# Strassen's seven block products for the output projection of a two-layer decoder trunk

## Chip, cores and metric

The kernel runs on one core of a Trainium2 chip. The metric is the device time of one launch in microseconds; the median of three runs of the kernel before is 1445.24 us. Its hardware profile is of one more execution, which took 1446.19 us.

## What is computed

Two layers of a hybrid decoder trunk on 1024 tokens with 1024 channels, all in float32: a norm, one wide input projection, sliding-window attention with sinks and a gated linear recurrence beside each other, a gated merge, an output projection and a residual addition; then a final norm. What matters here is the end of each layer:

```
merged = (jax.nn.sigmoid(gate_attn) * (a @ w_up_attn[layer])
          + jax.nn.sigmoid(gate_hgrn) * (b @ w_up_hgrn[layer]))
x = x + merged @ w_out[layer]
...
return rms_norm(x, final_norm_w)
```

`a` and `b` are 1024 x 512 each, `merged` is 1024 x 1024, `w_out[layer]` 1024 x 1024.

## The kernel before

Every large product is computed in a split form: an operand is rounded by ScalarE to a shorter float (`hi`, a cast to float32r), VectorE subtracts to get the rest (`lo`), and TensorE adds three products, lo x hi, hi x lo and hi x hi, into one accumulator. So a product costs three matmuls for each block of 128 of the contraction, and each operand piece costs one cast on ScalarE and one subtraction on VectorE. `split_w` (L125) writes the two parts into buffers with two copies each, `split_slot` (L333) into slots. There are 40 slots of 4 KB per partition (`slot`, tag "slot"), which most tiles of the kernel share. Accumulators come from two pools of PSUM banks: three under the tag "pj", five under "bank". Loads and most stores are issued by SyncE's queue, in order.

The kernel is written in a framework that inserts the semaphores and orders each engine's instructions itself: the order of the program text is the priority, and work that is ready earlier may go ahead of work that stands before it.

The input projection already uses seven block products (`combine`, `pair_first`, `pair_rest`). Its results for the gates are written through the activation to the DRAM tensor `gd`. While the recurrence runs, `filling` (L1039) feeds TensorE with independent work, the last part of which is `up_attn` (L811): for pairs of 128 output channels it computes `a @ w_up_attn` for both halves of the tokens, copies the accumulators to `u1` with ScalarE, loads the first branch's gates (`gate_in`) and multiplies on VectorE.

The merge (L1073 to L1089) then runs over four pairs of channel blocks: it loads and splits the weights of the second up projection (`up_chunk`, L788), loads the second gates into `u2`, and for each channel block and each half of the tokens computes 12 matmuls (`up`, L793), multiplies the accumulator by the gate (L802), adds `u1` (L1084), and writes `hi` (L1086) and `lo` (L1087) into `mg`. `mg[a][k]` is half `a` of the tokens, channel block `k`, with channels on partitions: the stationary operand of the output projection.

The output projection differs between the layers. In both, an accumulator holds 128 tokens x 512 output channels and sums 8 channel blocks, thus 24 matmuls:

- Layer 0 (L1143 to L1174): for each half of the tokens and each half of the output channels, four accumulators are open; pieces of `w_out` of 256 rows are loaded, split, and used by all four. Each piece of `w_out` is loaded and split twice, once for each half of the tokens. Then the residual is added (L1168), and the rows are stored to `xd`. The first half's norm for the next layer (`norm_scale`, `norm_turn`: squares on ScalarE, a short chain and a scaling on VectorE, transposes on TensorE, copies, casts and low parts) stands after the first two accumulations of the second half, and three chunks of the next layer's input weights (`first_chunk`) are loaded within it.
- Layer 1 (L1098 to L1142): all of `w_out` is split once. After a first round over the four first blocks, each block of 128 tokens is completed in turn (`part`, L1102), its residual added and squared (`add`, L1112), and `finish` (L1119) computes the final norm's factor, scales and stores.

Of the kernel before, what the change touches and what calls it, by code (L numbers as in the profile page):

```python
# [10 lines left out]
F32 = mybir.dt.float32  # L11
# [6 lines left out]
P = 128  # L18
# [20 lines left out]
def trunk_kernel(ctx, tc, x, positions, norm_w, w_in, attn_sinks, hgrn_norm_w, w_up_attn,  # L39
# [432 lines left out]
    for L in range(DEPTH):  # L472
# [331 lines left out]
        def gate_in(c, nm):  # L804
            t = slot([P, T], nm)
            nc.sync.dma_start(t, gd[c * P:(c + 1) * P])
            return t
# [3 lines left out]
        def up_attn(m, asp):  # L811
            w = up_chunk(w_up_attn[L], m, f"ua{L}_{m}")
            u1.extend(slot([P, T], f"u1_{L}_{m + j}") for j in range(2))
            n = 0
            for j in range(2):
                for a in range(2):
                    up(a, j, w, asp, u1[m + j][:, a * 512:(a + 1) * 512], f"ua{L}_{m + j}_{a}", True)
# [5 lines left out]
            for j in range(2):  # L823
                t = gate_in(m + j, f"ga_{L}_{m + j}")
                V.tensor_tensor(out=u1[m + j], in0=u1[m + j], in1=t, op=ALU.mult)
# [247 lines left out]
        mg = [[None] * KT for _ in range(2)]  # L1073
        u2s = []
        for m in range(0, KT, 2):
            w = up_chunk(w_up_hgrn[L], m, f"uh{L}_{m}")
            u2s += [gate_in(KT + c, f"u2_{L}_{c}") for c in range(len(u2s), min(m + 4, KT))]
            u2 = u2s[m:m + 2]
            for j in range(2):
                for a in range(2):  # L1080
                    t = slice(a * 512, (a + 1) * 512)
                    u = u2[j][:, t]
                    up(a, j, w, bsp, u, f"uh{L}_{m + j}_{a}")
                    V.tensor_tensor(out=u, in0=u, in1=u1[m + j][:, t], op=ALU.add)  # L1084
                    g = slot([P, 2, 512], f"mg_{L}_{m + j}_{a}", F32R)
                    S.copy(g[:, 0], u)  # L1086
                    V.tensor_tensor(out=g[:, 1], in0=u, in1=g[:, 0].bitcast(F32), op=ALU.subtract)  # L1087
                    mg[a][m + j] = g


        last = L == DEPTH - 1

        def load_wo(n, nm):
            return split_rows(w_out[L], n * 512, 512, f"o{L}_{n}_{nm}", 0 if n else 4)

        if last:
            wo = [load_wo(0, "l")]
            xns = [load_x(b, L) for b in range(4)]  # L1098
            wo.append(load_wo(1, "l"))
            wb = bcast_row(final_norm_w, "fnw")  # L1100

            def part(b, n, acc, ks):  # L1102
                a, o = b // 4, (b % 4) * P
                for k in ks:
                    lh, ll = mg[a][k][:, 0, o:o + P], mg[a][k][:, 1, o:o + P]
                    PE.matmul(acc, lhsT=ll, rhs=wo[n][k][0], start=k == 0, stop=False)
                    PE.matmul(acc, lhsT=lh, rhs=wo[n][k][1], start=False, stop=False)
                    PE.matmul(acc, lhsT=lh, rhs=wo[n][k][0], start=False, stop=k == KT - 1)

            sums = {}  # L1110

            def add(b, n, acc):  # L1112
                xn = xns[b][:, n * 512:(n + 1) * 512]
                V.tensor_tensor(out=xn, in0=acc, in1=xn, op=ALU.add)
                if n == 0:
                    sums[b] = st.tile([P, 2], F32, tag="fs", name=f"fs_{b}", bufs=5)
                S.activation(junk[:, n * 512:(n + 1) * 512], xn, AF.Square, accum_out=sums[b][:, n:n + 1])

            def finish(b):  # L1119
# [96 lines left out]
```

## Time and profile before

| | |
|---|---|
| median of 3 runs | 1445.24 us (1443.05 to 1448.75) |
| profiled execution | 1446.19 us, of which the span of instructions is 1444.4 us |
| TensorE busy | 1415.8 us, 98% of the span |
| VectorE busy | 922.1 us, 64% |
| ScalarE busy | 691.1 us, 48% |
| merge, layer 0 / layer 1 | 598 to 641 us / 1305.6 to 1349 us |
| output projection, layer 0 / layer 1 | 641 to 733 us / 1349 to 1437.1 us |
| after the last matmul | 1437.1 to 1444.4 us |

In rows of groups, a line number is that of the kernel printed above; then come the engine, the operation, the tile written and the tiles read, the shape and the count, and behind the bar the busy time in us, the mean duration of one in ns, and the idle time of the engine just before them with what ended it. In rows of instructions in order of time, the first number is the start and the second the duration in us; what stands in brackets is the idle time before and what ended it. PE is TensorE, PEld its weight loads, DVE VectorE, ACT ScalarE, POOL GpSimd, SP SyncE. The time of a matmul overlaps that of the next.

### The profile page before, as it was taken

Reading aid. Unit: us, or ns where it says so; the run is one execution under the profiler, and the core shown is the slowest. Engines: PE = TensorE matmul, PEld = TensorE weight load, DVE = VectorE, ACT = ScalarE, POOL = GpSimd, SP = SyncE. Lnnn points to the kernel's source line nnn. Section 1 sums busy time; section 2 is a strip of 40 time slices with the busy share of each in tenths; the row PEclk is TensorE's granted clock in tenths of the full one; section 3 lists DMA queues with packets and bytes.
Section 4 is the critical chain, followed back from the end, with each engine's and each line's share of the span. In section 5 each row is a group of like instructions: output and inputs, shape, how many; then the busy total and the mean of one; then the engine's idle time right before and its main releaser. Section 6 shows DMA issues by size and latency. Waiting matters only on the chain.

```text
span 1444.4 us, 21317 instructions
## 1 busy us (share of the span) xinstructions
PE 1415.8 (98%) x8252; PEld 1149.4 (80%) x8252; DVE 922.1 (64%) x1560; ACT 691.1 (48%) x1382; POOL 68.6 (5%) x77
## 2 busy tenths in 40 slices
PE   8999999999999999999999999999999999999997
PEld 7877878878777878888888878887788778888886
DVE  5856756646645889673656466666456388978643
ACT  8754333245775644432556332333467655453321
POOL 1100000310000000000000000003000000000000
PEclk9999999999999999999999999999999999999999
DMA  8433443464236653355455343426523366443431
GB/s 271 155 109 124 142 151 123 145 164 133 71 113 202 218 190 130 139 181 170 156 199 154 102 131 124 142 92 199 170 77 105 125 206 225 155 174 133 144 134 59
DMA packets 194277, 214.35 MB, mean 148 GB/s; under 512 B 12480, under 2 KB 142016, under 8 KB 194176
## 3 DMA queue, kind: packets, MB, share of 16 engines
q1 hardware_dynamic: 161152, 161.59, 35.1%
q10 hardware_dynamic: 31488, 46.15, 8.7%
q0 software_dynamic: 1536, 5.24, 0.9%
q8 instruction: 65, 1.06, 0.3%
q14 instruction: 36, 0.29, 0.1%
HBM read 145.58 MB, written 59.77 MB: 142 GB/s over the span
## 4 chain that ended last, share of the span: by engine, by line
PE 78%; DVE 7%; ACT 6%; DMA 5%; issue 2%; SPq 0%; ACTq 0%; DVEq 0%
PE pb L291 4%; PE pb L293 4%; PE pb L292 4%; PE pg L263 3%; PE pg L265 3%; PE pc L291 3%; PE pg L264 3%; PE pc L293 2%; PE pc L292 2%; PE pj_qh L139 2%; PE pj_qh L141 2%; PE pj_qh L140 2%; PE av L746 2%; PE pj_f L139 2%; PE pj_f L140 2%; PE pj_f L141 2%
## 5 line engine op out<-in xcount | busy, mean ns | idle before, releaser
L128 ACT CAST whi_s<-ws 128x1024 fp32r<-128x1024 f32 x26 | 27.4, 1054 | 123.3 <-DVE ws L278 108.4
L706 DVE COPY_PREDICATED pr<-upper,sc 128x256 f32<-128x256 int32 x56 | 23.4, 444 | 51.6 <-ACT pr L705 43.9
L721 ACT ACTIVATE pr<-pr,mx 128x128 f32<-128x128 f32 x128 | 50.1, 396 | 5.0 <-DVE mx L718 4.0
L139 PE MATMUL pu_ua<-wh_a,wlo_ua 128*128 128x512 f32 x128 | 52.2, 408 | 0.0
L141 PE MATMUL pu_ua<-wh_a,whi_ua 128*128 128x512 f32 x128 | 50.7, 396 | 0.0
L1164 PE MATMUL po<-wlo_o,mg 128*128 128x512 f32 x128 | 49.9, 390 | 0.7 <-DVE wlo_o L129 0.7
L483 ACT ACTIVATE pq<-pq 128x512 f32<-128x512 f32 x60 | 37.7, 631 | 26.3 <-DVE pq L303 25.1
L263 PE MATMUL pg<-hh,wlo_p 128*128 128x512 f32 (+1 forms) x128 | 47.0, 372 | 3.3 <-POOL wlo_p L129 1.5
L140 PE MATMUL pu_ua<-wl_a,whi_ua 128*128 128x512 f32 x128 | 50.2, 392 | 0.0
L1163 PE MATMUL po<-whi_o,mg 128*128 128x512 f32 x128 | 49.9, 390 | 0.0
L1165 PE MATMUL po<-whi_o,mg 128*128 128x512 f32 x128 | 49.8, 389 | 0.0
L139 PE MATMUL pu_uh<-wh_b,wlo_uh 128*128 128x512 f32 x128 | 49.8, 389 | 0.0
L140 PE MATMUL pu_uh<-wl_b,whi_uh 128*128 128x512 f32 x128 | 49.8, 389 | 0.0
L141 PE MATMUL pu_uh<-wh_b,whi_uh 128*128 128x512 f32 x128 | 49.8, 389 | 0.0
L303 DVE TENSOR_TENSOR pq<-pb,p 128x512 f32<-128x512 f32 x40 | 27.6, 690 | 31.9 <-PE pb L293 31.8
L264 PE MATMUL pg<-hl,whi_p 128*128 128x512 f32 (+1 forms) x128 | 46.1, 363 | 0.0
L265 PE MATMUL pg<-hh,whi_p 128*128 128x512 f32 (+1 forms) x128 | 46.0, 363 | 0.0
L1086 ACT CAST mg<-u 128x512 fp32r<-128x512 f32 x32 | 19.8, 621 | 51.3 <-DVE u L1084 51.3
L277 DVE TENSOR_TENSOR ws<-wr 128x512 f32<-128x512 f32 x26 | 17.9, 690 | 39.5 <-DMA wr<-in_w_in_dram 39.5
L263 PE MATMUL pg<-hh,wl_p 128*128 128x512 f32 (+1 forms) x112 | 41.2, 369 | 1.8 <-DVE wl_p L337 1.2
L291 PE MATMUL pb<-th,wl 128*128 128x512 f32 x104 | 41.3, 397 | 1.7 <-DVE pq L303 1.7
L129 DVE TENSOR_TENSOR wlo_t<-ws,whi_t 128x1024 fp32r<-128x1024 f32 x26 | 31.8, 1223 | 16.5 <-ACT whi_t L128 16.5
(391 smaller groups left out, 4432.6 us busy)
## 6 DMA issues: line engine op xcount, KB each, us to landing
wr<-in_w_in_dram SPq DMA_DIRECT2D x64, 512.0 KB
gd<-pq ACTq DMA_DIRECT2D x76, 256.0 KB
wr_p<-in_w_in_dram SPq DMA_DIRECT2D x26, 512.0 KB
fq<-fq ACTq DMA_DIRECT2D x48, 256.0 KB
x<-in_x_dram SPq DMA_DIRECT2D x16, 512.0 KB
ga<-gd SPq DMA_DIRECT2D x16, 512.0 KB
u<-gd SPq DMA_DIRECT2D x16, 512.0 KB
wr_o<-in_w_out_dram SPq DMA_DIRECT2D x16, 512.0 KB
```

What stands on the lines that cost most here:

```text
L139: PE.matmul(acc, lhsT=ll, rhs=rh, start=i == 0, stop=False)
L140: PE.matmul(acc, lhsT=lh, rhs=rl, start=False, stop=False)
L141: PE.matmul(acc, lhsT=lh, rhs=rh, start=False, stop=i == n - 1)
L263: PE.matmul(acc, lhsT=wl[:, k], rhs=h[:, t], start=k == 0, stop=False, skip_group_check=q > 0)
L264: PE.matmul(acc, lhsT=wh[:, k], rhs=l[:, t], start=False, stop=False, skip_group_check=q > 0)
L265: PE.matmul(acc, lhsT=wh[:, k], rhs=h[:, t], start=False, stop=k % 4 == 3, skip_group_check=q > 0)
L291: PE.matmul(acc, lhsT=wl[:, k], rhs=h, start=start and k == 0, stop=False, skip_group_check=not start)
L292: PE.matmul(acc, lhsT=wh[:, k], rhs=l, start=False, stop=False, skip_group_check=not start)
L293: PE.matmul(acc, lhsT=wh[:, k], rhs=h, start=False, stop=k == 3, skip_group_check=not start)
L721: S.activation(pr[:, h], pr[:, h], AF.Exp, bias=mx[:, h:h + 1], accum_out=sm[:, h:h + 1])
L1163: PE.matmul(accs[j], lhsT=ll, rhs=wh[:, i], start=k + i == 0, stop=False)
L1164: PE.matmul(accs[j], lhsT=lh, rhs=wl[:, i], start=False, stop=False)
```

## The change

The output projection of both layers becomes one routine. The merged matrix A (tokens x channels) and W = `w_out` are cut into halves both ways, and the four blocks of the result are formed from seven products of 512 x 512 blocks in Winograd's arrangement, with the sums S1 = A21 + A22, S2 = S1 - A11, S3 = A11 - A21, S4 = A12 - S2 and T1 = B12 - B11, T2 = B22 - T1, T3 = B22 - B12, T4 = T2 - B21 (up to sign and order of writing). (The code writes S3 as A22 - S2, and T4 as B21 - T2.) Each product takes four row blocks, four channel blocks and three matmuls each, 48 matmuls. Products go in the order 1, 2, 6, 5, 3, 7, 4 and accumulate in two sets of four banks, X and Y; the residual rows are added from a bank after each stage that completes a term of an output block (`add`), so that a block of the output is built up in `xns` by several additions, and X or Y goes on accumulating.

The sums are VectorE operations on tiles of 128 x 1024, in place. Operands are split when their product comes up: the left ones into slots, the right ones into the two buffers of `split_w`, but for product 4, whose right operand goes to slots and whose matmuls run block by block, so that each block's rows are complete at the block's end. `w_out` is loaded once as eight tiles of 256 rows x 512 columns, during the merge.

In the merge, `up` writes into tiles of two channel blocks x 512 tokens; the addition of the two branches is one operation for two channel blocks; no split is made there. The multiplication of `u1` by the first branch's gates moves from `up_attn` into the merge, with its loads, and both kinds of gates are loaded by half of the tokens.

In layer 0, the first half's norm now stands ahead of product 4, and two of the three early weight chunks behind it. In layer 1, the first four blocks are finished ahead of product 4 (`finish_block`), the other four within it. The list `weighed` is empty, so both halves of a block are scaled by VectorE.

```
--- before.py
+++ after.py
 
 
-        def up_chunk(w, m, nm):
+        def up_load(w, m, nm):
             raw = wp.tile([P, 4, 2 * P], F32, tag="wraw", name=f"wr_{nm}")
             nc.sync.dma_start(raw, w[:, m * P:(m + 2) * P].rearrange("(k p) c -> p k c", p=P))
-            return split_w(raw, nm, [P, 4, 2 * P])
+            return raw
+
+        def up_chunk(w, m, nm):
+            return split_w(up_load(w, m, nm), nm, [P, 4, 2 * P])
 
         def up(a, j, w, src, dst, nm, wait=False):
 
...
-            nc.sync.dma_start(t, gd[c * P:(c + 1) * P])
+        def gate_in(c, a, nm):
+
+            t = slot([P, 2, 512], nm)
+            nc.sync.dma_start(t, gd[c * P:(c + 2) * P].rearrange("(j p) t -> p j t", p=P)[:, :, a * 512:(a + 1) * 512])
             return t
 
         u1 = []
 
         def up_attn(m, asp):
             w = up_chunk(w_up_attn[L], m, f"ua{L}_{m}")
-            u1.extend(slot([P, T], f"u1_{L}_{m + j}") for j in range(2))
+            u1.append([slot([P, 2, 512], f"u1_{L}_{m}_{a}") for a in range(2)])
             n = 0
             for j in range(2):
                 for a in range(2):
-                    up(a, j, w, asp, u1[m + j][:, a * 512:(a + 1) * 512], f"ua{L}_{m + j}_{a}", True)
+                    up(a, j, w, asp, u1[m // 2][a][:, j], f"ua{L}_{m + j}_{a}", True)
                     n += 1
                     if n == 1:
                         yield
                     elif n == 2:
                         yield
-            for j in range(2):
-                t = gate_in(m + j, f"ga_{L}_{m + j}")
-                V.tensor_tensor(out=u1[m + j], in0=u1[m + j], in1=t, op=ALU.mult)
             yield
 
...
-        mg = [[None] * KT for _ in range(2)]
+
+        mg = [[], []]
         u2s = []
+        last = L == DEPTH - 1
+
+        def w_block(q, n):
+
+            res = []
+            for kp in (2 * q, 2 * q + 1):
+                t = slot([P, 2, 512], f"wo_{L}_{n}_{kp}")
+                nc.sync.dma_start(t, w_out[L][kp * 2 * P:(kp + 1) * 2 * P, n * 512:(n + 1) * 512]
+                                  .rearrange("(k p) c -> p k c", p=P))
+                res.append(t)
+            return res
+
+        wo = {}
+        raws = [up_load(w_up_hgrn[L], 0, f"uh{L}_0")]
         for m in range(0, KT, 2):
...
+            w = split_w(raws.pop(0), f"uh{L}_{m}", [P, 4, 2 * P])
+            if m + 2 < KT:
+                raws.append(up_load(w_up_hgrn[L], m + 2, f"uh{L}_{m + 2}"))
+            for c in range(2 * len(u2s), min(m + 4, KT), 2):
+                u2s.append([(gate_in(KT + c, a, f"u2_{L}_{c}_{a}"), gate_in(c, a, f"ga_{L}_{c}_{a}")) for a in range(2)])
+            for a in range(2):
+                u, t = u2s[m // 2][a]
+                V.tensor_tensor(out=t, in0=t, in1=u1[m // 2][a], op=ALU.mult)
+                for j in range(2):
+                    up(a, j, w, bsp, u[:, j], f"uh{L}_{m + j}_{a}")
+                V.tensor_tensor(out=u, in0=u, in1=t, op=ALU.add)
+                mg[a].append(u)
+            if m:
+                for q, n in (((0, 0),), ((0, 1), (1, 0)), ((1, 1),))[m // 2 - 1]:
+                    wo[q, n] = w_block(q, n)
+
...
+        a11, a12, a21, a22 = mg[0][:2], mg[0][2:], mg[1][:2], mg[1][2:]
+        b11, b12, b21, b22 = wo[0, 0], wo[0, 1], wo[1, 0], wo[1, 1]
+        X = [pj.tile([P, 512], F32, tag="pj", name=f"px_{L}_{j}") for j in range(3)] + [bank([P, 512], f"px_{L}_3")]
+        xns = []
+        def sums(out, in0, in1, op):
+            for o, i0, i1 in zip(out, in0, in1):
+                V.tensor_tensor(out=o, in0=i0, in1=i1, op=op)
+        def split_a(a, nm):
+            return [split_slot(t, f"m{L}_{nm}_{i}", [P, 2, 512]) for i, t in enumerate(a)]
+        def product(acc, a, w, nm, start, by_block=False, first=None):
+            ws = []
+            for kp in range(2):
+                ws.append(w[kp] if by_block else split_w(w[kp], f"o{L}_{nm}_{kp}", [P, 2, 512]))
+                for j in [] if by_block else range(4):
+                    times(acc[j], a[kp], ws[kp], j, start, kp)
+            for j in range(4) if by_block else []:
+                first(j)
+                for kp in range(2):
+                    times(acc[j], a[kp], ws[kp], j, start, kp)
+                yield j
+        def times(acc, a, w, j, start, kp):
+            for i in range(2):
+                lh, ll = a[0][:, i, j * P:(j + 1) * P], a[1][:, i, j * P:(j + 1) * P]
+                PE.matmul(acc, lhsT=ll, rhs=w[0][:, i], start=start and kp + i == 0, stop=False,
+                          skip_group_check=not start)
+                PE.matmul(acc, lhsT=lh, rhs=w[1][:, i], start=False, stop=False, skip_group_check=not start)
+                PE.matmul(acc, lhsT=lh, rhs=w[0][:, i], start=False, stop=kp + i == 2, skip_group_check=not start)
+        def run(*args):
+            for _ in product(*args):
+                pass
+        ssq, weighed = {}, []
+        def add(acc, a, n, done=False, js=range(4)):
+            for j in js:
+                b = 4 * a + j
                 xn = xns[b][:, n * 512:(n + 1) * 512]
+                V.tensor_tensor(out=xn, in0=acc[j], in1=xn, op=ALU.add)
+                if last and done:
+                    if b not in ssq:
+                        ssq[b] = st.tile([P, 2], F32, tag="fs", name=f"fs_{b}", bufs=8)
+                    S.activation(junk[:, n * 512:(n + 1) * 512], xn, AF.Square, accum_out=ssq[b][:, n:n + 1])
+        def finish_block(b):
+            V.tensor_tensor(out=ssq[b][:, 0:1], in0=ssq[b][:, 0:1], in1=ssq[b][:, 1:2], op=ALU.add)
+            r = rsqrt(ssq[b][:, 0:1], 1, 1.0 / D, f"fin_{b}", True)
+            for n in range(2):
+                c = slice(n * 512, (n + 1) * 512)
+                if n and b in weighed:
+                    S.activation(xns[b][:, c], xns[b][:, c], AF.Copy, scale=r)
+                else:
                     V.scalar_tensor_tensor(out=xns[b][:, c], in0=xns[b][:, c], scalar=r, in1=wb[:, c],
                                            op0=ALU.mult, op1=ALU.mult)
+                nc.sync.dma_start(out[0, b * P:(b + 1) * P, c], xns[b][:, c])
+        m11 = split_a(a11, "11")
+        run(X, m11, b11, "1", True)
+        xns += [load_x(b, L) for b in range(4)]
+        m12 = split_a(a12, "12")
+        Y = [bank([P, 512], f"py_{L}_{j}_0") for j in range(4)]
+        run(Y, m12, b21, "2", True)
+        sums(a21, a21, a22, ALU.add)
+        sums(a11, a21, a11, ALU.subtract)
+        sums(b11, b12, b11, ALU.subtract)
+        t2 = [slot([P, 2, 512], f"t2_{L}_{i}") for i in range(2)]
+        sums(t2, b22, b11, ALU.subtract)
+        add(X, 0, 0)
+        m = split_a(a11, "s2")
+        run(X, m, t2, "6", False)
+        sums(a12, a12, a11, ALU.subtract)
+        add(Y, 0, 0, True)
+        xns += [load_x(b, L) for b in range(4, NB)]
+        m = split_a(a21, "s1")
+        Y = [bank([P, 512], f"py_{L}_{j}_1") for j in range(4)]
+        run(Y, m, b11, "5", True)
+        add(X, 0, 1)
+        if last:
+            wb = bcast_row(final_norm_w, "fnw")
         else:
             wb = bcast_row(norm_w[L + 1], f"nw_{L + 1}")
             hT, hF, early = HT(f"{L + 1}"), Turned(f"{L + 1}"), []
+        m = split_a(a12, "s4")
+        add(Y, 1, 1)
+        run(Y, m, b22, "3", False)
+        sums(b12, b22, b12, ALU.subtract)
+        sums(a11, a22, a11, ALU.subtract)
+        m = split_a(a11, "s3")
+        run(X, m, b12, "7", False)
+        sums(b21, b21, t2, ALU.subtract)
+        m22 = split_a(a22, "22")
+        w4 = split_a(b21, "t4")
+        add(Y, 0, 1, True)
+        if not last:
+            early.append(first_chunk(L + 1, 0, True))
+            for b in range(4):
+                nc.sync.dma_start(xd[b * P:(b + 1) * P], xns[b])
+            norm_turn(norm_scale(xns[:4], wb, f"n{L + 1}_0"), hT, hF, 0, f"n{L + 1}_0")
+        if last:
+            for b in range(4):
+                finish_block(b)
+        for j in product(X, m22, w4, "4", False, True, lambda j: add(X, 1, 1, True, [j])):
+            add(X, 1, 0, True, [j])
+            if last:
+                finish_block(4 + j)
+            else:
+                nc.sync.dma_start(xd[(4 + j) * P:(5 + j) * P], xns[4 + j])
+        if not last:
+            early += [first_chunk(L + 1, j, True) for j in (1, 2)]
+            xnl = xns[4:]
```

More of the change, by code (lines that the diff above doesn't have):

```diff
@@ L1070, in trunk_kernel @@
             pass
-        mg = [[None] * KT for _ in range(2)]
+        mg = [[], []]
         u2s = []
-        for m in range(0, KT, 2):
[L1076 to L1088, printed above, removed]
```

73 lines of the change are left out of this document (removed).

## Prediction

> **What bounds the kernel now.** I read the shares of the engines first, then the stretches around the change (layer 0 and layer 1: merge, output projection, what follows), then the order of TensorE's instructions, and last what VectorE does there.
>
> ```profile
> PE 1415.8 (98%) x8252; PEld 1149.4 (80%) x8252; DVE 922.1 (64%) x1560; ACT 691.1 (48%) x1382; POOL 68.6 (5%) x77
> PE 78%; DVE 7%; ACT 6%; DMA 5%; issue 2%; SPq 0%; ACTq 0%; DVEq 0%
> ```
>
> ```profile
> 598.00:641.00 43.00, 43.00 (x191) 35.59 (x190) 36.64 (x52) 14.19 (x22) 0.00 (x0) 1.00 0.42 135
> 641.00:733.00 92.00, 91.30 (x420) 75.79 (x419) 46.44 (x58) 35.39 (x54) 0.00 (x0) 1.00 0.51 164
> 1305.60:1349.00 43.40, 43.40 (x193) 35.92 (x193) 36.82 (x53) 14.42 (x22) 0.00 (x0) 1.00 0.29 97
> 1349.00:1437.10 88.10, 87.45 (x385) 71.78 (x383) 37.41 (x82) 21.35 (x46) 0.00 (x0) 1.00 0.35 126
> 1437.10:1444.40 7.30, 0.00 (x0) 0.00 (x0) 3.06 (x9) 0.93 (x3) 0.00 (x0) 0.72 0.19 72
> ```
>
> The columns are length, then busy time of PE, PEld, DVE, ACT, POOL, the granted clock, the DMA share and GB/s. Rows one and three are the two merges, two and four the two output projections, five the end. TensorE is busy throughout all four, at clock 1.00; VectorE is busy 85% of a merge, but only 50% and 42% of the projections. So TensorE is the bound, and VectorE has half of the projections free. That free half is what the change spends.
>
> A matmul's 389 ns overlaps the next one's, so its price is the distance between starts:
>
> ```profile
> 701.06 0.39 PE L1164 MATMUL po<-wlo_o,mg 128*128 128x512 f32 x1
> 707.41 0.39 PE L1165 MATMUL po<-whi_o,mg 128*128 128x512 f32 x1
> 707.64 3.65 PE L225 MATMUL tp_n<-ident,x 128*128 128x128 f32 x32
> 711.05 0.48 PE L1163 MATMUL po<-whi_o,mg 128*128 128x512 f32 x1
> ```
>
> 28 steps in 6.35 us: 0.227 us each. A projection has 384 (8 row blocks, 2 column halves, 8 blocks of the contraction, 3 terms of the split), thus 87.05 us. From 641.3 to 732.7 the first projection takes 91.4; less 87.05 and the 3.4 of 32 transposes that sit in it (707.64 to 711.05), about 1.0 is idle.
>
> ```profile
> L1106 PE MATMUL po<-whi_o_l,mg x32: 389/389/389, 1349.0 to 1428.1; 128*128 128x512 f32 x32
> L1108 PE MATMUL po<-wh_o_l,mg x96: 388/389/398, 1360.3 to 1436.7; 128*128 128x512 f32 x96
> L1163 PE MATMUL po<-whi_o,mg x128: 389/389/476, 641.3 to 732.2; 128*128 128x512 f32 x128
> ```
>
> The second runs from 1349.0 to 1436.9, 87.9, with 0.9 idle.
>
> **The change part by part.** **Matmuls removed.** Seven products of 4 row blocks x 4 blocks of the contraction x 3 terms are 336 instead of 384: 48 fewer per layer, 96 in all, of the same 128x512 shape with a weight load each. 96 x 0.227 = -21.8 us, all on the path. The Trainium skill (TensorE: Matmul & The Clock Gate, "Wait — 56ns, not 53.3ns?") gives 215.7 ns start to start for such a matmul; that would be -20.7, and the row above decides for 0.227.
>
> **VectorE work added to the projection.** The rows for the prices:
>
> ```profile
> 756.55 1.22 DVE L337 TENSOR_TENSOR wl_p<-wr_p,wh_p 128x1024 fp32r<-128x1024 f32 x1
> 757.68 1.22 DVE L241 TENSOR_TENSOR h<-h,h 128x1024 f32<-128x1024 f32 x1
> 758.82 1.22 DVE L240 TENSOR_TENSOR h<-h,h 128x1024 f32<-128x1024 f32 x1
> L1168 DVE TENSOR_TENSOR x<-po,x 128x512 f32<-128x512 f32 x16 | 10.7, 687 | 5.6 <-PE po L1165 5.6
> L128 ACT CAST whi_o<-wr_o 128x1024 fp32r<-128x1024 f32 x16 | 17.0, 1060 | 46.6 <-PE po L1165 33.4 <-DMA wr_o<-in_w_out_dram 12.1 <-PE pu_uh L141 1.1
> ```
>
> A 128x1024 subtraction or sum lasts 1.22, but where nothing is awaited the next one starts 1.14 later; I take 1.15. Per layer: 14 operand pieces of each side (seven products, two tiles each) make 28 low parts; eight sums of two tiles make 16; together 44 x 1.15 = 50.6. Seven sets of four additions from PSUM are 28 x 0.66 = 18.5. Sum 69. Three of the first product's four low parts fit in the merge. ScalarE gets 28 casts x about 1.0 = 28 for a projection of 76 us, and is no bound.
>
> Set against this, product by product, with 0 at the first product (10.9 us each on TensorE, order 1, 2, 6, 5, 3, 7, 4). The hard point is the third: products 1 and 2 last 21.8 us, and before product 6 VectorE owes two low parts of a12, two of b21, eight sums and two low parts of S2, one of T2 (15 x 1.15 = 17.3) and four additions from PSUM (2.6): 19.9. The last merge operand comes some 2 us late (0.69 + 1.22 behind the last matmul), so 19.9 stand against 19.8, less what went ahead in the merge (a12's pieces come free before its end). Products 5, 3 and 7 owe less than the 10.9 of one product each: four low parts with two sums and four additions, with eight additions, or with four sums are 9.2 to 9.9, and the sums can go ahead. Up to product 4 I take +1.5 per layer for stalls at operands; bounds 0 and, if the third product waits for its chain in a row (two sums, a cast and a low part, 1.23 + 1.23 + 1.06 + 1.23), 4.8.
>
> Weight pieces keep two buffers each, freed per half product (24 matmuls, 5.4 us); cast and low part take 2.3 of that. w_out is now read once (8 loads of 512 KB, not 16, in layer 0), ahead of use, and the waits for it go: the 1.0 and 0.9 idle above, -1.9.
>
> **Merge.** It loses 16 additions and 16 low parts of 128x512 (about 21 us by these rows):
>
> ```profile
> L1084 DVE TENSOR_TENSOR u<-u,u 128x512 f32<-128x512 f32 x16 | 10.9, 688 | 0.3
> L1087 DVE TENSOR_TENSOR mg<-u,mg 128x512 fp32r<-128x512 f32 x16 | 10.9, 688 | 3.7 <-ACT mg L1086 3.4
> L825 DVE TENSOR_TENSOR u<-u,ga x16: 1209/1214/1220, 542.9 to 1309.3; 128x1024 f32<-128x1024 f32 x16
> ```
>
> and gains eight wide additions and eight gate products (16 x 1.15 = 18.4): no more than now, and under the 43.4 of its matmuls. Six of the eight gate products per layer came before the merge, where TensorE was busy too; nothing is gained by their leaving (0; bound -1 per layer). Their loads (4 MB) move into the merge with w_out's 4 MB, 4 MB of the second gates and 2 MB of weights: at most 14 MB in 43 us, 325 GB/s, and less as the first gates go ahead of it. In the stretch 1200 to 1445, in slices of 6.1 us:
>
> ```profile
> GB/s 255 228 375 53 80 217 175 248 268 3 0 96 319 101 6 371 312 31 58 102 155 196 64 86 2 226 402 114 364 163 104 88 86 0 86 39 49 86 0 86
> ```
>
> Single slices reach 371 and 402, so I take 0 and keep 3 per layer as the bound. On SyncE's queue these loads stand behind waits for weight buffers, which come free every 10.9 us; two groups of gates go ahead.
>
> **End of layer 0.** The first half's norm now has its inputs only after product 3, two products (21.8 us) before the projection ends; so far its transposes ran 21 us before the end with inputs ready at 685. Ahead of product 4 VectorE owes one weight piece, a chain of 12 short operations and four scalings:
>
> ```profile
> 689.32 0.16 DVE L108 TENSOR_SCALAR ms_n<-ss_n 128x4 f32<-128x4 f32 x1
> 691.71 3.67 DVE L170 SCALAR_TENSOR_TENSOR x<-x,y_n,nw 128x1024 f32<-128x1024 f32 x3
> 696.69 1.27 DVE L170 SCALAR_TENSOR_TENSOR x<-x,y_n,nw 128x1024 f32<-128x1024 f32 x1
> L231 ACT CAST hh<-h 128x1024 fp32r<-128x1024 f32 x8 | 8.1, 1186 | 0.0
> L232 DVE TENSOR_TENSOR hl<-h,hh 128x1024 fp32r<-128x1024 f32 x8 | 9.3, 1220 | 11.5 <-ACT hh L231 11.5
> ```
>
> Product 3 ends at 54.5, squares to 60, short chain to 62.5, scalings to 67.5; product 7 ends at 65.3, the transposes (3.4) fill to about 68.7, and the additions that free product 4's accumulators come at 67.5 to 68. +1.0, bounds 0 and 5 (all scalings exposed). Copies, casts and low parts are done by 77, product 4 at 80: layer 1 starts without a gap. Its second half is needed only some 60 us later.
>
> **End of layer 1.** The finishing of a block:
>
> ```profile
> 1436.69 0.39 PE L1108 MATMUL po<-wh_o_l,mg 128*128 128x512 f32 x1
> 1437.12 0.69 DVE L1114 TENSOR_TENSOR x<-po,x 128x512 f32<-128x512 f32 x1 [4.75 <-PE po L1108]
> 1438.66 0.16 DVE L1120 TENSOR_TENSOR fs<-fs 128x1 f32<-128x1 f32 x1 [0.85 <-ACT junk L1117]
> 1439.86 0.16 DVE L122 SCALAR_TENSOR_TENSOR y_fin<-yt_fin,y_fin 128x1 f32<-128x1 f32 x1
> 1440.06 1.41 DVE L1124 SCALAR_TENSOR_TENSOR x<-x,y_fin,fnw 128x512 f32<-128x512 f32 x2
> ```
>
> Six short operations at 0.195 and the pair of 1.41 are 2.6 of VectorE per block. Blocks 0 to 3 stand in the program ahead of product 4's first additions: 55.5 + 10.3 = 66 against 65.3, +1.5 before product 4 starts (bounds 0 and 5). There each block costs VectorE 0.69 + 2.6 = 3.3, TensorE 12 x 0.227 = 2.7: 0.6 x 3 of backlog on the end, +1.7 (bounds 0 and 4). The last chain (4.35) and store (1441.5 to 1444.4) stay.
>
> **Sum** against the profiled execution's own 1446.19 (span 1444.4): -21.8 - 1.9 + 3.0 (stalls at operands) + 1.0 + 1.5 + 1.7 = -16.5, 1429.7. The median of the runs, 1445.24, lies 0.95 lower: 1428.7 us, 1.1% faster. (0.5%, or 7 us, is about what a measurement tells from no change.)
>
> **Rivals.** **VectorE becomes the bound.** In layer 1 it owes 69 - 3.5 + 8 x 2.6 = 86 from the first product to the end, where TensorE's 76.2 and the last chain's 4.4 are 80.6. The merge, with 4 x 1.15 + 18.4 + 16 x 0.66 = 33.6 of its 43.4, has 6 free for sums of w_out's blocks and a12's pieces, which brings it just under. Where little goes ahead and each wait on TensorE leaves a hole, I put 5 more in layer 1 and 4 in layer 0: 1437 to 1438. For it: a load near 100%. Against: most sums wait for nothing but each other. The Trainium skill (VectorE: DVE Perf Modes, "The DRAIN you can't avoid") says that the next operation isn't started before the pipe is empty, with a start-to-start gap for each; its section on two instructions with no wait between them allows an earlier start. By the first rule each 1.15 would be 1.22 and each layer owes 3 us more, which brings about this rival; the rows at 756.55 and 757.68 speak for the second. The nearest case, the block products of the input projection, speaks against long stalls:
>
> ```profile
> PE pb L291 <- DVE pq L303: 0.7, 3, 0.3
> 800.00:880.00 80.00, 79.26 (x347) 64.06 (x346) 49.05 (x68) 28.16 (x38) 0.00 (x0) 1.00 0.39 125
> ```
>
> (the first row over 800 to 1040 us), though VectorE is at 61% there.
>
> **Slots run out (slower).** Splits, sums, T2, x and w_out now share the 40 slots. I count 34 to 38 in product 6, 39 at the end of layer 0. If the next product's pieces can't be written before the last one's are freed, each of 12 later products exposes its chain of about 4.8: 58 - 24 = +34, 1479. It decides (slower by 7) from (24 + 7) / 12 = 2.6 us per product. Against: my counts stay under 40.
>
> **Only half is gained.** Gates or w_out land late in the merge, TensorE waits for accumulators that VectorE can't empty: 3 us per layer, and the two ends cost double (4 more): 1438 to 1441, within 0.5%.
>
> **How the numbers follow.** Forecast 0.58 (own range 1420 to 1435: all stalls zero with 1 per layer gained before the merge, to nearly double their sum of 7.2); VectorE as the bound 0.22, three quarters of it below 1438; half gained 0.12; slots 0.08, of which most lies over 1452. Faster by over 0.5%: 0.58 + 0.17 + 0.05 = 0.80; within: 0.12; slower: 0.08. The range 1420 to 1440 leaves about 1 in 10 above and few below.
>
> **What would show it.** 672 projection matmuls, not 768, at 0.227; VectorE over 85% busy in both projections; TensorE's waits for low parts at product 6 and for the additions at product 4 near 1 us each; merges of 43 to 44 us; the end 7 to 9 us behind the last matmul. I'm wrong if TensorE waits over 5 us at a product's start, if the merge grows, or if VectorE's idle time in the projection waits for slots or loads.

## Result, and the profile after

The changed kernel takes 1424.24 us (median of 4 runs, 1423.11 to 1425.52), the kernel before 1444.38 in the same comparison: a ratio of 0.9856, 95% interval 0.9832 to 0.988, so 20.1 us or 1.4% less. The profiled execution took 1423.34 us; its span is 22.8 us shorter than before. Below are the page's head of the changed kernel (engine shares, then the shares of the chain that ended last) and its stretches (length, busy time of PE, PEld, DVE, ACT, POOL, granted clock, DMA share, GB/s), cut at the same places as before: the two merges, the two projections, the end.

```profile
span 1421.6 us, 21133 instructions
PE 1394.7 (98%) x8156; PEld 1131.5 (80%) x8156; DVE 981.7 (69%) x1600; ACT 701.3 (49%) x1382; POOL 72.1 (5%) x77
PE 81%; DVE 7%; ACT 6%; DMA 3%; issue 1%; SPq 0%; ACTq 0%; DVEq 0%
```

```profile
596.50:640.00 43.50, 43.50 (x194) 36.01 (x193) 36.68 (x40) 7.25 (x9) 0.00 (x0) 1.00 0.81 297
640.00:720.40 80.40, 80.30 (x370) 66.31 (x369) 75.53 (x90) 42.15 (x60) 0.00 (x0) 1.00 0.22 81
1292.50:1336.00 43.50, 43.50 (x194) 36.02 (x193) 36.69 (x40) 7.20 (x9) 0.00 (x0) 1.00 0.71 275
1336.00:1412.10 76.10, 76.10 (x337) 62.81 (x335) 72.87 (x112) 37.46 (x62) 0.00 (x0) 1.00 0.17 66
1412.10:1421.60 9.50, 0.15 (x1) 0.00 (x0) 6.40 (x23) 1.15 (x5) 0.00 (x0) 0.74 0.43 166
```

The merges have not changed (43.5 us each, before as after). Layer 0's projection went from 91.4 to 80.4 (-11.0), layer 1's from 87.9 to 76.1 (-11.8), and the end behind the last matmul grew from 7.5 to 9.5 (+2.0). That is -20.8 of the span's -22.8. Of the rest, 1.3 lies ahead of layer 0's merge, where matmuls are the same, and 0.7 between the layers; single executions differ by that much.

VectorE is now busy for 75.53 of 80.40 us (94%) and 72.87 of 76.10 (96%), against 50% and 42% before. What do both engines wait for? First TensorE's waits from 600 to 1320 us (the two longest rows), then VectorE's in layer 0's projection (engine, line, who is waited for: total, times, longest):

```profile
PE pj_z L139 <- DVE wlo_z L129: 2.0, 1, 2.0
PE tb L1022 <- DVE tab L1013: 0.7, 1, 0.7
```

```profile
DVE hl L232 <- ACT hh L231: 2.5, 2, 2.4
DVE x L1152 <- PE px L1139: 1.2, 3, 0.7
DVE wlo_o L129 <- ACT whi_o L128: 0.6, 1, 0.6
```

No row of TensorE names `px` or `py`, the accumulators of the block products, and from 1320 us to the end TensorE's list is empty. VectorE's waits in layer 0's projection come to 4.3 us. Two engines run side by side, both almost without a pause. The starts of product 4 and of layer 1 in TensorE's order show it too (start, duration, line, tiles):

```profile
705.08 0.39 PE L1139 MATMUL px<-whi_o,wh_m_s 128*128 128x512 f32 x1
705.30 0.39 PE L1136 MATMUL px<-wh_m_t,wl_m 128*128 128x512 f32 x1
...
720.15 0.39 PE L1139 MATMUL px<-wh_m_t,wh_m 128*128 128x512 f32 x1
720.38 0.39 PE L263 MATMUL pg<-hh,wl_p 128*128 128x512 f32 x1
```

Both hand-overs take the ordinary step of 0.22 to 0.23 us.

### The profile page after: what moved, and what is told of

It reads as the page before. It is cut to its first block, busy times and chain, and to the rows that moved or that the text cites. A ratio compares the mean times of both kernels' runs of the same rounds, so it can differ in the third digit from the quotient of the medians.

```text
span 1421.6 us, 21133 instructions
## 1 busy us (share of the span) xinstructions
PE 1394.7 (98%) x8156; PEld 1131.5 (80%) x8156; DVE 981.7 (69%) x1600; ACT 701.3 (49%) x1382; POOL 72.1 (5%) x77
## 4 chain that ended last, share of the span: by engine, by line
PE 81%; DVE 7%; ACT 6%; DMA 3%; issue 1%; SPq 0%; ACTq 0%; DVEq 0%
PE pb L291 4%; PE pb L293 4%; PE pb L292 4%; PE pc L291 3%; PE pc L293 3%; PE pc L292 3%; PE pg L263 3%; PE pg L265 2%; PE pg L264 2%; PE pj_qh L139 2%; PE pj_qh L141 2%; PE pj_qh L140 2%; PE av L746 2%; PE pu_uh L141 2%; PE pu_uh L140 2%; PE pu_uh L139 2%
## 5 line engine op out<-in xcount | busy, mean ns | idle before, releaser
L128 ACT CAST whi_o<-wo 128x1024 fp32r<-128x1024 f32 x20 | 21.1, 1055 | 77.0 <-PE pu_uh L141 35.5
L303 DVE TENSOR_TENSOR pq<-pb,p 128x512 f32<-128x512 f32 x40 | 27.6, 689 | 31.9 <-PE pb L293 31.7
L139 PE MATMUL pj_z<-hh,wlo_z 128*128 128x512 f32 x96 | 38.5, 401 | 4.1 <-DVE wlo_z L129 4.1
L291 PE MATMUL pc<-hh,wlo_t 128*128 128x512 f32 x104 | 41.2, 396 | 0.0
L291 PE MATMUL pb<-th,wlo_s 128*128 128x512 f32 x104 | 40.9, 393 | 0.0
```

Of the source, the lines that this page charges most:

```text
L128: S.copy(hi, raw)
L139: PE.matmul(acc, lhsT=ll, rhs=rh, start=i == 0, stop=False)
L291: PE.matmul(acc, lhsT=wl[:, k], rhs=h, start=start and k == 0, stop=False, skip_group_check=not start)
```

## Experiments

Differences to the changed kernel are between medians of different comparisons; in all of them the kernel before took 1444.4 to 1445.1. The theory: TensorE sets the length, and VectorE's added work fits beside it with almost nothing left over, because much of it runs ahead of its place. The main rival: VectorE sets the pace already, and fewer matmuls, or less work on VectorE, would show it.

**Each layer alone.** The merge and projection of the changed kernel in one layer, those of before in the other.

```
+        if L == 0:                      # second kernel: L == 1
             ...                         # merge and projection as changed
+        else:
+            ...                         # merge and projection of before
```

> The seven products and the new merge in layer 0 alone; layer 1 as before. Theory (the gain is the 48 matmuls per layer at 0.227 us, all of VectorE's new work hidden): 10.9 less for matmuls and 1 for the old waits, 11 to 12 us below the kernel before, about 1433. Rival (much of the gain comes from layer 1, or from the gates' move): 5 to 8 us below.

> The seven products and the new merge in layer 1 alone; layer 0 as before. Theory: 11.8 less up to the last matmul, 2.0 more behind it, 9 to 10.5 us below the kernel before, about 1434.5; with the run for layer 0 it adds up to the whole gain. Rival (the layers help each other, or the gain lies elsewhere): the two sums differ from the whole by more than 4 us.

Layer 0 alone: 1435.41 us, 0.9934 (0.9921 to 0.9946), 9.2 less. Layer 1 alone: 1434.04, 0.9926 (0.9914 to 0.9939), 10.5 less. Together 19.7, where the whole change gave 20.1: no help or hindrance between the layers shows. Layer 1 gave what was expected. Layer 0 gave about 2 us less than the 11 to 12 of the theory; 11 would lie within its interval, 12 just outside.

**The gates' move alone, in the kernel before.**

```
-                V.tensor_tensor(out=u1[m + j], in0=u1[m + j], in1=t, op=ALU.mult)       # up_attn
+                V.tensor_tensor(out=u1[m + j], in0=u1[m + j], in1=gas[m + j], op=ALU.mult)  # merge
```

> Only the first branch's gate products move into the merge, in both layers; the projection is as before. Theory: TensorE is busy on both sides of the move, so 0, within 2 us of the kernel before. Rival (VectorE is relieved in the recurrence, where it is 87% busy, and the chain through it gets shorter): 3 to 5 us faster. Second rival (the merge gets too much for VectorE or the loads): 3 or more slower, seen as a merge longer than 43.5 us.

1447.6 us, 1.002 (1.0011 to 1.0029): 3.0 us slower. The theory (within 2 us) and the first rival missed; the time is that of the second rival. By itself the move brings no gain. Of that rival's sign, a longer merge, a part shows. TensorE has a wait that the kernel before doesn't have, once in each merge, for the low part of the next weights:

```profile
PE pu_uh L139 <- DVE wlo_uh L129: 1.5, 2, 0.7
```

That is 1.5 of the 3.0. The profiled span is 1444.6, as before, but each is that of one execution; where the rest lies stays open.

**The gates put back, in the changed kernel.**

```
+            for a in range(2):                                       # end of up_attn
+                t, u = gate_in(m, a, f"ga_{L}_{m}_{a}"), u1[m // 2][a]
+                V.tensor_tensor(out=u, in0=u, in1=t, op=ALU.mult)
...
-                V.tensor_tensor(out=t, in0=t, in1=u1[m // 2][a], op=ALU.mult)   # merge
```

> The changed kernel with the products by the first branch's gates put back ahead of the merge (block products as they are). VectorE then has 8 x 1.15 = 9 us less to do in each merge, of which TensorE waits for none. Theory (the move is worth nothing either way where the merge is TensorE's): within 1.5 us of the changed kernel's 1424, the merges still 43.5 us. Rival: the move costs what it cost by itself (3.0 us slower than before), and taking it back gains that: 1421, seen as shorter stretches ahead of or in the merge. Second rival: the room that it leaves in the merge lets sums go ahead, and the end behind the last matmul falls by 1 to 2 us, to 8: 1422 to 1423.

1433.67 us, 0.9919 (0.9906 to 0.9933): 9.4 slower than the changed kernel, and all three expectations missed it. Two rows of stretches place the loss, first the changed kernel from the end of one projection to the next merge, then this one:

```profile
720.40:1292.40 572.00, 567.01 (x3445) 455.85 (x3444) 365.89 (x595) 287.09 (x577) 31.45 (x29) 1.00 0.45 144
```

```profile
726.90:1304.00 577.10, 568.55 (x3445) 457.04 (x3444) 367.49 (x599) 286.13 (x577) 33.84 (x29) 1.00 0.47 150
1304.00:1423.70 119.70, 119.70 (x529) 98.92 (x528) 105.56 (x150) 44.94 (x71) 0.00 (x0) 1.00 0.31 113
1423.70:1432.40 8.70, 0.18 (x1) 0.00 (x0) 4.93 (x18) 1.02 (x4) 0.00 (x0) 0.75 0.47 181
```

Layer 1's merge and projection keep their 119.7 us, and the end is 0.8 shorter. The time is lost ahead of the merges, where the recurrence ends: this stretch is 5.1 us longer, and layer 0's merge starts 7.2 later (603.7 against 596.5). There, in layer 0, with the gates back, VectorE's order and then TensorE's are (a number in brackets is idle time before the instruction, and what ended it):

```profile
562.30 2.35 DVE L829 TENSOR_TENSOR u<-u,ga 128x1024 f32<-128x1024 f32 x2
...
565.00 0.69 DVE L874 TENSOR_TENSOR R<-R,tab 128x512 f32<-128x512 f32 x1
...
567.42 0.69 DVE L874 TENSOR_TENSOR R<-R,tab 128x512 f32<-128x512 f32 x1
...
568.40 1.21 DVE L129 TENSOR_TENSOR wlo_ua<-wr_ua,whi_ua 128x1024 fp32r<-128x1024 f32 x1
```

```profile
564.21 0.52 PE L945 MATMUL lv_m<-gs,R 128*32 128x48 f32 x32
568.16 1.07 PE L963 MATMUL l<-Q,R 128*32 128x32 f32 x32 [3.43 <-DVE R L874]
569.67 0.79 PE L139 MATMUL pu_ua<-wh_a,wlo_ua 128*128 128x512 f32 x1 [0.44 <-DVE wlo_ua L129]
570.26 0.63 PE L140 MATMUL pu_ua<-wl_a,whi_ua 128*128 128x512 f32 x1
570.69 0.63 PE L141 MATMUL pu_ua<-wh_a,whi_ua 128*128 128x512 f32 x1
```

```profile
568.00:574.00 6.00, 5.40 (x42) 4.40 (x43) 5.83 (x19) 0.72 (x2) 3.46 (x4) 0.50 0.29 93
```

A pair of gate products (2.35 us) stands ahead of the recurrence's chain, and the low part of the next weights, which would have let TensorE go on with `pu_ua`, stands behind it, at 568.40; in the changed kernel that subtraction runs at 559.08. Neither a load nor ScalarE held it back, as the cast of these weights ran at 543.2. TensorE has nothing to do for 3.43 us, and then runs at a granted clock of 0.50 to about 574.5 (matmuls 0.43 us apart, not 0.227). Layer 1 has the same 3.43. Twice 3.43, 0.4 and 0.8 for the low part, and 2.5 and 1.7 from the clock (12 and 9 matmuls, 0.2 more each) make 12.3 us, as much as the 7.2 and 5.1 together. Layer 0's merge and projection (123.2 us) and the end are 0.7 and 0.8 shorter, so the spans differ by 10.8; the medians differ by 9.4. So the block products without the move give 11.4 us of the 20.1. But what is lost is the price of an order on VectorE's queue: the kernel before multiplies at the same place (561.14, 2.35 us) and has no such wait, because there the low part went ahead, at 560.01. That the move must precede the block products isn't shown; another order with the gates back wasn't tried.

**VectorE's work in program order.** The sums, low parts and residual additions of the projection may no longer run ahead of what stands before them.

```
-                V.tensor_tensor(out=o, in0=i0, in1=i1, op=op)
+                keep(V.tensor_tensor(out=o, in0=i0, in1=i1, op=op))   # keep: in program order
```

> The changed kernel with VectorE's splits, sums and additions of the output projection held in the order of the program text; nothing else is changed. Theory (the new work is hidden because it is done ahead of its product, in VectorE's idle time): TensorE then waits for operands at the first product (5.5), the third (6.8) and the sixth accumulation (1.9), about 14 us per layer, 28 in all, about 1452. Rival (order hardly matters, since VectorE has time enough in each product): 0 to 4 us slower than the changed kernel, 1424 to 1428.

1510.35 us, 1.0447 (1.0429 to 1.0466): 86 us slower than the changed kernel. The theory had the direction and under a third of the size. TensorE's longest waits from 600 us on, and the stretch around layer 1's last products:

```profile
PE px L1138 <- DVE x L1154: 33.8, 5, 11.4
PE px L1138 <- DVE wl_m_s L337: 8.5, 2, 4.3
PE tp_n L225 <- DVE x L170: 7.4, 1, 7.4
```

```profile
1392.00:1508.00 116.00, 77.30 (x293) 60.37 (x291) 77.28 (x129) 35.16 (x62) 0.00 (x0) 0.83 0.11 41
```

The waits for low parts, which the theory was about, come to some 18 us in both layers (8.5 above, 6.4 for `wl_m`, and 3.4 for `wlo_o`), less than its 28. The largest wait is for the additions that free accumulators (33.8, of which 26.5 in layer 1's product 4), which my figure left out: in program order they stand behind the whole finishing of the blocks before, and in layer 0 behind the norm of the first half. The waits cost the clock as well (0.83 here). So running ahead is not a detail: without it the change would lose far more than the matmuls save. But the 86 us are the price of all of it together, of the additions above all.

**More of VectorE's work.** 14 low parts computed twice, 16 us, in one layer.

```
+            for t, (hi, lo) in zip(a, res) if L == 0 and nm != "t4" else []:    # then L == 1
+                V.tensor_tensor(out=lo, in0=t, in1=hi.bitcast(F32), op=ALU.subtract)
```

> The changed kernel with the low parts of the left operands computed twice in layer 0: 14 more VectorE operations of 128x1024 at 1.15 us, 16 us. Theory (VectorE at the edge; its lead and the little idle time eat 2 to 4): 12 to 14 us slower than the changed kernel, 1436 to 1438, with waits of TensorE at the last product and at layer 1's first gates. Rival (the lead of 9 us that the last product's operands have covers most of it): 0 to 5 us slower.

> The same in layer 1: 16 us more of VectorE. Theory (from the fifth product to the end VectorE works without a pause, and the end follows VectorE): 13 to 15 us slower than the changed kernel, 1437 to 1439, as a longer stretch behind the last matmul and waits before it. Rival (hidden by the lead): 0 to 5 us slower.

In layer 0: 1442.46, 0.9977 (0.9967 to 0.9986), 18.2 slower than the changed kernel, more than the 12 to 14 expected. In layer 1: 1437.35, 0.995 (0.9933 to 0.9966), 13.1 slower, as expected. The rows are merge and projection together, which take 123.9 and 119.7 in the changed kernel: layer 0 of the first kernel, layer 1 of the second.

```profile
597.20:735.50 138.30, 128.56 (x561) 103.94 (x561) 126.97 (x142) 48.24 (x69) 0.00 (x0) 0.98 0.38 140
```

```profile
1292.50:1423.90 131.40, 123.14 (x527) 99.25 (x527) 122.94 (x158) 44.88 (x71) 0.00 (x0) 0.99 0.32 121
```

16 us more on VectorE lengthen them by 14.4 and 11.7, and the end in layer 1 by 1.8 more. Behind layer 0 the stretch to the next merge grows as well, by 4.1 (576.1 against 572.0). A part of this is the clock: in layer 0 TensorE is busy for 128.56 us, against 123.80 for the same matmuls. VectorE had about 2 us to spare per layer at most (1.6 and 2.5 by these figures).

**Fewer matmuls, fewer low parts, and both.** Three kernels answer the rival from the other side.

```
+                if few:                      # product 5: 8 of 48 matmuls stay
+                    if i:
+                        PE.matmul(acc, lhsT=ll, rhs=w[1][:, i], start=kp == 0, stop=kp == 1)
+                    continue
...
+        if not low:                          # operands of products 5, 3 and 7
+            return hi, hi
```

> The changed kernel with 8 of the 48 matmuls of the fourth product in order (product 5), in both layers; so that product is left out but for its accumulators' writes, and VectorE's work is unchanged. Removed: 80 x 0.227 = 18.1 us. Theory (VectorE stands at the edge in both projections, 94% to 96% busy, so the next matmuls removed no longer pay): 4 to 7 us below the changed kernel, 1417 to 1420, with TensorE waiting for low parts. Rival (TensorE alone is the bound): 16 to 18 us below, 1406 to 1408.

> Of the changed kernel, the low parts of the operands of products 5, 3 and 7 are left out in both layers (their matmuls stay, and read the high part instead): 12 subtractions of 128x1024 per layer, 12 x 1.15 = 13.8 us of VectorE, fewer. The output is then not the reference's. Theory (TensorE sets the length, VectorE runs just under it): no wait of TensorE is there to go, so the projections stay at 80.4 and 76.1 us, and only the backlog at the end goes: the stretch behind the last matmul falls from 9.5 to about 7.3, the time by 2 to 2.5 us, to 1422 where the changed kernel gave 1424. Rival (VectorE sets the length, and TensorE's steady row is only as fast as VectorE feeds it): the projections shorten too, by 5 us or more per layer: 1414 or less.

> The same 12 low parts per layer left out, and with them the 40 matmuls of product 5 per layer that the kernel with fewer matmuls left out (2 x 40 x 0.227 = 18.1 us of TensorE); the output is not the reference's. By itself that removal of matmuls made the changed kernel 3.2 us slower. Theory (there VectorE, without a pause, had become the bound): with both gone VectorE has about 62 us of work in layer 0's 71 and 59 in layer 1's 67, so the matmuls' 18.1 now show: 1424 - 18 - 2 = 1404, between 1402 and 1408. Rival (what held that kernel back was the order of the buffers or the loads, which are the same here): TensorE waits as there, and the time stays at 1420 to 1427.

| left out, both layers | time (us) | ratio to before | against the changed kernel |
|---|---|---|---|
| 80 matmuls (18.1 us) | 1427.43 | 0.9881 (0.9864 to 0.9897) | +3.2 |
| 24 low parts (27.6 us) | 1423.01 | 0.9847 (0.9831 to 0.9863) | -1.2, within the spread |
| both | 1406.89 | 0.9728 (0.9715 to 0.9741) | -17.4 |

Merge and projection of layer 0, then of layer 1, for the three in that order:

```profile
595.30:718.10 122.80, 119.37 (x521) 96.55 (x520) 109.39 (x126) 47.17 (x67) 0.00 (x0) 0.97 0.43 157
718.10:1295.70 577.60, 568.85 (x3446) 457.07 (x3445) 368.84 (x597) 289.24 (x578) 31.45 (x29) 1.00 0.44 143
1295.70:1413.90 118.20, 114.65 (x489) 92.97 (x487) 108.58 (x149) 44.80 (x71) 0.00 (x0) 0.97 0.36 138
```

```profile
595.60:718.80 123.20, 123.20 (x561) 102.54 (x560) 101.30 (x119) 49.70 (x69) 0.00 (x0) 1.00 0.41 153
1290.60:1410.30 119.70, 119.70 (x529) 98.88 (x527) 98.73 (x147) 44.77 (x72) 0.00 (x0) 1.00 0.37 141
1410.30:1419.40 9.10, 0.12 (x1) 0.00 (x0) 5.71 (x15) 0.93 (x3) 0.00 (x0) 0.75 0.45 173
```

```profile
597.40:712.60 115.20, 114.69 (x521) 94.87 (x520) 100.94 (x119) 49.50 (x69) 0.00 (x0) 1.00 0.44 162
1285.20:1396.90 111.70, 111.19 (x489) 91.25 (x487) 97.83 (x147) 44.69 (x72) 0.00 (x0) 1.00 0.39 151
```

9.07 us fewer matmuls alone shorten the two stretches by 1.1 and 1.5, with TensorE idle for 3.4 and 3.6 of them and the clock at 0.97, so that the matmuls that are left take longer; layer 1 then begins with a wait (2.8 us, for `wl_p`), and the stretch between the layers is 5.6 longer (second row). Low parts alone change the stretches by 0.7 and nothing. Only both together bring 8.7 and 8.0 of the 9.07, and the time that the theory gave (1402 to 1408). So neither engine alone sets the length: they are level, and a gain needs both. (A low part left out also shortens the chain from cast to matmul. That VectorE's time counts, and not this chain, is argued from its 94% to 96% and from the 16 us above; no run separates the two.) The theory's figure for fewer matmuls (4 to 7 less) was wrong in sign, and its 7.3 us for the end with fewer low parts as well: the end stayed at 9.1.

**The end: finishing of blocks 0 to 3 moved off VectorE**, to ScalarE and GpSimd.

```
+                    S.activation(xns[b][:, c], xns[b][:, c], AF.Copy, scale=r)
+                    G.tensor_tensor(out=xns[b][:, c], in0=xns[b][:, c], in1=wb[:, c], op=ALU.mult)
```

> The changed kernel; the final norm of blocks 0 to 3 is scaled on ScalarE (by the row's factor) and GpSimd (by the weights) instead of VectorE: eight pairs leave VectorE, 5.6 us. Theory (the 2.0 us that the stretch behind the last matmul grew by is VectorE's backlog): that stretch goes back from 9.5 to 7.5 us, the time falls by 2, about 1422. Rival (GpSimd's 2.8 us for a tile of 128x1024, or its use of the same memory, holds something up): 0 to 2 us slower.

1428.09 us, 0.988 (0.9865 to 0.9894): 3.9 slower, where the theory had 2 faster and the rival 0 to 2 slower, and the end grew from 9.5 to 12.6. The timeline shows GpSimd's products and, while they run, VectorE's short operations:

```profile
1402.06 7.53 POOL L1165 TENSOR_TENSOR x<-x,fnw 128x512 f32<-128x512 f32 x6 [136.29 <-ACT x L1164]
...
1405.12 0.17 DVE L113 RECIPROCAL y_fin<-yt_fin 128x1 f32<-128x1 f32 x1 [1.91 <-ACT yt_fin L112]
...
1405.84 1.28 DVE L120 TENSOR_TENSOR yt_fin<-y_fin 128x1 f32<-128x1 f32 x1
...
1408.40 1.21 DVE L122 SCALAR_TENSOR_TENSOR y_fin<-yt_fin,y_fin 128x1 f32<-128x1 f32 x1
```

A two-input operation on one column, 0.16 us in the changed kernel, takes 1.2 to 1.3, about the 1.26 of one GpSimd product; three of them cost 3.2 us more. VectorE also waits 1.91 us for a square root that stands on ScalarE behind six of the new scalings (3.79 us). From 1336 us to the end VectorE is busy for 79.3 us, as long as in the changed kernel, though eight scalings have left it. So this run couldn't show whether the end is VectorE's backlog.

## Why the prediction was right, and which terms were off

The forecast was 1428.7 and the time 1424.2, within the forecast's own range. By its steps:

- **Matmuls removed, -21.8; old waits, -1.9.** Right. 336 matmuls at 0.2266 us fill layer 1's 76.1 without a gap; in layer 0 they leave 4.3 of the 80.4 to the transposes. The stretches' -11.0 and -11.8 are these two terms together with the +0.8 of the end of layer 0 below.
- **Stalls at operands, +3.0; start of product 4 in layer 1, +1.5.** These are the mis-sized terms: TensorE waits for neither, 0 and 0, and not the "near 1 us each" that was to show it. The step that failed is the account product by product, with VectorE at 19.9 against 19.8 at product 6 and at 66 against 65.3 at product 4, and with an allowance on top: the account itself was short by only 0.1 and 0.7. It let work run ahead only between neighbours and out of the merge. The timeline of VectorE shows it running further ahead:

```profile
633.92 1.21 DVE L1116 TENSOR_TENSOR u<-u,u 128x1024 f32<-128x1024 f32 x1
635.66 1.21 DVE L1116 TENSOR_TENSOR wo<-wo,wo 128x1024 f32<-128x1024 f32 x1
...
1389.88 2.35 DVE L337 TENSOR_TENSOR wl_m_t<-wo,wh_m_t 128x1024 fp32r<-128x1024 f32 x2
...
1397.33 0.69 DVE L1152 TENSOR_TENSOR x<-px,x 128x512 f32<-128x512 f32 x1
1398.69 0.69 DVE L1152 TENSOR_TENSOR x<-px,x 128x512 f32<-128x512 f32 x1 [0.67 <-PE px L1139]
1400.12 4.07 DVE L1166 SCALAR_TENSOR_TENSOR x<-x,y_fin,fnw 128x512 f32<-128x512 f32 x6
1404.16 0.68 DVE L1152 TENSOR_TENSOR x<-px,x 128x512 f32<-128x512 f32 x1
```

  Two of the sums from which product 6's operands are built (L1116) are done inside the merge. The last low part that the start of product 6 needs then ends at 660.99, 0.8 us ahead of its first matmul (661.78); in layer 1 it is 0.8 as well. The last operand of product 4 is ready at 1392.2, 9 us before its first matmul at 1401.2. Two of the four additions that free accumulators for product 4 slip in ahead of the finishing, which the program places before them; the other two come at 1404 behind six scalings (4.07), in time for the third block, which TensorE reaches at 1401.2 + 24 x 0.227 = 1406.6. In the kernel kept in program order TensorE waits some 18 us for low parts and 33.8 for additions that free accumulators.
- **End of layer 0, +1.0.** About 0.8, but not as one wait for the norm. The 32 transposes add up to 3.3 us (3.4 before), but run in four groups of eight, as VectorE's four scalings release them from 706.71 on, 1.2 us apart; one matmul runs between, and the changes cost 0.1 to 0.25 each, 0.8 in all:

```profile
708.05 1.09 PE L225 MATMUL tp_n<-ident,x 128*128 128x128 f32 x8
708.90 0.48 PE L1139 MATMUL px<-wh_m_t,wh_m 128*128 128x512 f32 x1
709.25 1.09 PE L225 MATMUL tp_n<-ident,x 128*128 128x128 f32 x8
```

  The hand-over itself, 720.15 to 720.38, has no gap, and the first half's norm (its last low parts end at 720.97) came just in time.
- **Backlog at the end, +1.7.** Measured +2.0; the end of 9.5 lies outside the 7 to 9 that were to show it. The kernel with fewer low parts leaves 9.1 of the 9.5, though in it the finishing of blocks 0 to 3 is over at 1397.0, ahead of product 4 (1399.4), and VectorE has time left in product 4 (one wait of 2.03 for TensorE). So the delay arises within product 4, by its own finishing, as the term said, and most of it isn't carried over.
- **Merge, 0; the gates' move, 0 with a bound of -1 per layer.** The merge stayed at 43.5 us, so its 0 holds, loads of 297 GB/s included. The move's 0 to -1 did not: by itself the move costs 3.0 us, and beside the block products taking it back loses 9.4. This term was put at nothing because TensorE is busy on both sides of the move; it left out that the order on VectorE's queue changes with it.
- **VectorE over 85% busy.** Right, at 94% and 96%. The rival that VectorE becomes the bound was given 0.22, with 86 us owed in layer 1 from the first product on, less 6 in the merge. The rows above give 72.87 + 6.40 = 79.3: about 6.7 went ahead, and against the 80.6 it came out just on the forecast's side of that rival. With 1.3 us between the two, and TensorE and VectorE level by the runs above, this is partly luck. In the Trainium skill (VectorE: DVE Perf Modes, "The DRAIN you can't avoid") no operation starts before the last has drained; two low parts in 2.35 us, not 2 x 1.22, again agree with the page's section on two instructions with no wait between them. 3 us more per layer would have been more than the 2 or so to spare.
- **Slots run out; only half gained.** Neither occurred: TensorE waits for no slot, gate or piece of `w_out` in the projections, and the merges did not grow.

So the terms measure -21.8 - 1.9 + 0.8 + 2.0 = -20.9 where the forecast had -16.5: the two stall terms make -4.5 of the difference, the two ends +0.3 and -0.2. The forecast and the median differ by 4.5 as well, but that agreement is partly chance: the change of the medians is 20.1, 3.6 beyond the forecast's 16.5, and the other 0.9 is that the kernel before was faster in this comparison (1444.38 against 1445.24).

## What to carry to other kernels

Trading matmuls for additions pays only as long as the second engine has the time: count its work over the whole stretch, the stage before included, rather than product by product, since work whose operands exist early moves ahead by itself. A busy share of 96% doesn't say which engine is the bound; taking work from each alone and from both does. Where two engines are level, an order on one queue that leaves the other without filling work for 3 us costs nearly twice its length.

## What the hardware showed

- After 3.43 us without a matmul the granted clock was 0.50 for 6.7 us in layer 0 (567.8 to 574.5) and, from 1.8 us after the restart, for 3.4 us in layer 1 (1271.0 to 1274.4), and 128x512 matmuls started 0.43 us apart where 0.227 is usual; that a stall of 3.4 us grows to some 6 in this way was in none of my prices. The Trainium skill (TensorE: Matmul & The Clock Gate, "What's actually happening") states a half clock after an idle window of about 3.4 us; the trace agrees. For the way back the page gives a busy window of about 3.4 us that runs freely; layer 1's 3.4 agrees, layer 0's 6.7 is twice that.
- VectorE's two-input operations on one column took 1.2 to 1.3 us, not 0.16, while GpSimd multiplied 128x512 tiles in SBUF; one with a single input (0.17) and additions from PSUM (0.69) kept their time. The Trainium skill (SBUF — State Buffer, "Who interferes with whom") says that a VectorE instruction with two SBUF inputs contends with a GpSimd instruction that reads SBUF, and calls the port pair that they share an exclusive lock. The length of 1.2 to 1.3, one GpSimd product, agrees.
